# Residual combinations split in product order, a later token scale, and a residual added at the end of the down products

## The chip, the cores and the metric

One core of one Trainium2 chip runs the whole program. The metric is the device time of one execution in microseconds (us); of the kernel before, 3 runs give a median of 2325.0 us (2323.95 to 2326.51).

## What is computed

One layer of an encoder with two branches, for two requests of 256 tokens each (512 tokens in all), width 2048, all in float32. After the mixer (attention heads and a gated delta rule, together y) the layer is

```python
h  = h + mixed                      # mixed = y @ w_out
hn = rmsnorm(h, norm_ffn_w)
h  = h + (silu(hn @ w_gate) * (hn @ w_up)) @ w_down
return rmsnorm(h, final_norm_w)     # x * rsqrt(mean(x*x) + 1e-6) * w
```

with `w_gate` and `w_up` of 2048 x 5632 and `w_down` of 5632 x 2048. The change lies wholly behind the mixer: in the residual after `w_out`, the opening of the gate products, and the `w_down` stage with its residual.

## The kernel before, in words

Activations lie transposed: 128 features on the partitions, 512 tokens (T) along a row, 16 such row tiles for the 2048 features. L = 256 is one request's half of the row.

**Every float32 product is made of three.** A matrix is split into a high part (`hi`, a rounding on ACT, L126) and a low part (`lo`, the difference on DVE, L127). PE multiplies hi by hi, hi by lo and lo by hi. In the matmul rows of the profile `ps_g`, `ps_a` and so on name the PSUM bank, `w_hi` and `w_lo` the weights. All PE code runs in program order; DVE, ACT and POOL run in an order that a scheduler makes from the program order and from leads: code under `high_priority(offset=AHEAD)` is placed as if it stood 120 instructions earlier. The pools allow three raw weight tiles (`raw`), three `hi` and three `lo`, three PSUM banks of tag `g`, three of tag `s`, and one each of `o0` and `o1`.

**The residual stage (L852-877)** runs over 16 row tiles in the order 0, 8, 1, 9 and so on, so that tile j is followed by tile j + 8. Each gets its half of the `w_out` products, the residual is added (L858), the row is stored to memory as `s_h2` (L859), and it is scaled into four blocks (two feature halves by two token halves). From the four blocks seven inputs of a Strassen-like scheme are built: A11, A12, A22 are blocks, S1 to S4 sums and differences (L864-872). They stand in one tile `cmb`, and after row j + 8 all seven are split at once into `XC[j]` (L873, 1792 columns). L877 adds up the squares for the norm's scale.

**Gate and up products.** A block of two feature tiles needs seven products instead of eight: A11, S3, S1, A12, S2, S4, A22 in this order. Each runs over j = 0 to 7 with the eight tiles of `XC`, first all high weights and then all low ones. The weights of a product are blocks b11, b21, b22 of the matrix or their running sums (`first`, `second`, the first addition by an accumulating DMA of POOL, L914). The products A11 and A12 share the bank `ps_a`: between them a copy and an add (L896/L897) read A11 out as `p1`. There are 22 gate blocks and 22 up blocks, alternating. In the first gate block, `open_gate` (L982-994) runs after the product A11: one PE product that sums the squares over all features (`ps_s<-ssq_acc,ones`), a square root on ACT, four reciprocals on DVE (L202), each over 128 columns, and the opening of the pools in which the blocks hold their results. Each block ends with a multiplication by the scale (L977). The results of an up block are stored to memory by POOL (`s_act`, L1011), or kept split in `sA`.

**Down stage.** The 5632 inputs fall into three segments of plain products (`down`, L1041-1055), two groups that use the seven-product scheme (`down_group`, L1093), and a last segment (`down_half`, L1160), one token half after the other with the final norm behind it. The order is down(0), group 0, down(1), group 1, down(2), and the two halves. In `down` each j has one load of 512 KB of weights on SP's queue (`w_raw`), a split, and two row tiles of twelve matmuls; `tt(hk, hk, ps, add)` (L1051) adds the bank to the result's row of `hT`. Beside the j's, `combos` builds the group's inputs (`a_raw`, `a_sum`, split into `xd`). Before down(0) sixteen POOL loads bring the residual `s_h2` into `hT` (L1026-1027); `hT` takes memory that the gate and up blocks used until then, and a tile waits for the last user of its place. PE, DVE and ACT are in-order: what stands behind a waiting instruction waits too.

Of the kernel before, what the change touches and what calls it, by code (L numbers as in the profile page):

```python
# [8 lines left out]
F32 = mybir.dt.float32  # L9
F32R = mybir.dt.float32r  # L10
# [7 lines left out]
P = 128  # L18
# [43 lines left out]
def hybrid_encoder(ctx: ExitStack, tc: tile.TileContext, xT, w_in, w_ba, w_out, w_gate,  # L62
# [786 lines left out]
    st = st_cm.__enter__()  # L849
    acc = st.tile([P, T], F32, tag="acc", name="ssq_acc2")  # L850
    A11, A12, A22, S4, S3, S1, S2 = range(7)
    for n, i in enumerate(pairs):  # L852
        j = i % 8
        ps = pg.tile([P, T], F32, tag="g", name="ps_g")
        hk = st.tile([P, T], F32, tag="hk", bufs=2, name="hk")
        nc.sync.dma_start(hk, s_h1[i])
        half_gemm(ps, w_out[i, 1], dns, True, True)
        tt(hk, hk, ps, ALU.add)  # L858
        nc.gpsimd.dma_start(s_h2[i], hk)  # L859
        w = nwf[:, i:i + 1]  # L860
        if i < 8:
            cmb = st.tile([P, 7, L], F32, tag="cmb", name="cmb")
            a21 = st.tile([P, L], F32, tag="a21", name="a21")
            act(out=cmb[:, A11], in_=hk[:, :L], func=AF.Copy, scale=w)  # L864
            act(out=a21, in_=hk[:, L:], func=AF.Copy, scale=w)
            tt(cmb[:, S3], cmb[:, A11], a21, ALU.subtract)
        else:
            act(out=cmb[:, A12], in_=hk[:, :L], func=AF.Copy, scale=w)
            act(out=cmb[:, A22], in_=hk[:, L:], func=AF.Copy, scale=w)
            tt(cmb[:, S1], a21, cmb[:, A22], ALU.subtract)  # L870
            tt(cmb[:, S2], cmb[:, S1], cmb[:, A11], ALU.subtract)
            tt(cmb[:, S4], cmb[:, A12], cmb[:, S2], ALU.add)
# [45 lines left out]

    def block(src, f, pool, new_out, opened=None):


        with tc.high_priority(offset=3 * AHEAD):
# [19 lines left out]
        fp, out = state["fp"], new_out()  # L942
        p1 = fp.tile([P, L], F32, tag="p1", name="p1")
# [22 lines left out]
        tt(out[:, 3], out[:, 3], d[:, 1], ALU.add)  # L966
        with ahead():
# [3 lines left out]
        with ahead():  # L971
            tt(first, first, b21, ALU.add)
            w = w_split(first)
# [7 lines left out]

    def open_gate():  # L982
        ps = sm_tile()
        mm(ps, ones, acc, start=True, stop=True)
        rstd_bcast(ps, rstd2, st, 1)
        st_cm.__exit__(None, None, None)
        cp_cm.__exit__(None, None, None)
        sA_pool = ctx.enter_context(tc.tile_pool(name="sA", bufs=1, side="left",
                                                 reuse_waits="tile"))
        state["gb_cm"] = tc.tile_pool(name="gB", bufs=1, side="left", reuse_waits="tile")  # L990
        state["gB"] = state["gb_cm"].__enter__()
        state["fp_cm"] = tc.tile_pool(name="fp", bufs=1, side="left", reuse_waits="tile")
        state["fp"] = state["fp_cm"].__enter__()
        state["sA"] = sA_pool.tile([P, 2, SEG, T], F32R, tag="sA", name="aA")

    for p in range(NPAIR):
        g4 = block(w_gate, 2 * p, gA,
                   lambda: state["fp"].tile([P, 4, L], F32, tag="g4", name="ga"),
                   open_gate if p == 0 else None)
        act(out=g4, in_=g4, func=AF.Silu)  # L1000
        u4 = block(w_up, 2 * p, state["gB"],
                   lambda: state["fp"].tile([P, 4, L], F32, tag="u4", bufs=2, name="up"))
        tt(u4, u4, g4, ALU.mult)
        sA = state["sA"]
# [15 lines left out]
    ht = ctx.enter_context(tc.tile_pool(name="ht", bufs=1, side="left", reuse_waits="tile"))  # L1020
    hT = ht.tile([P, KT, T], F32, tag="h", name="hT")

    def hrow(i):
        return hT[:, i]

    for i in range(KT):  # L1026
        nc.gpsimd.dma_start(hrow(i), s_h2[i])
# [4 lines left out]
    sA = state["sA"]  # L1032

# [6 lines left out]

    def down(s, a, beside=()):  # L1041
        beside = list(beside)
        for j in range(8):
            wh, wl = load_w(w_down[s, j], [2, SEG, P])
            for i in range(2):
                ps = pg.tile([P, T], F32, tag="g", name="ps_g") if i == 0 else sm_tile()
                for k in range(SEG):
                    mm3(ps, wh[:, i, k], wl[:, i, k], a[:, 0, k], a[:, 1, k],
                        k == 0, k == SEG - 1)
                hk = hrow(2 * j + i)  # L1050
                tt(hk, hk, ps, ALU.add)  # L1051
            if beside:
# [39 lines left out]

    def down_group(g, X, sums, after):  # L1093
        plain = fetch_plain(g, 0)
        for j in range(8):
# [78 lines left out]
    def final_norm(b, acc):  # L1174
# [122 lines left out]
```

## Time and profile before

| | |
|---|---|
| median of 3 runs | 2325.0 us |
| profiled execution | 2323.5 us, span 2321.8 us, mean granted clock 0.993 |
| busy share of PE, DVE, ACT, POOL | 98%, 77%, 45%, 11% |
| HBM | 357.42 MB read, 36.00 MB written |
| mixer and residual stage | until about 968 us of the span |
| gate and up blocks | about 959 to 1835 us |
| down stage | about 1835 us to the end |

A row of the timeline gives the start and the busy time in us of one or more instructions on an engine (PE matrix products, PEld weight loads, DVE vector, ACT scalar, POOL and SPq the two queues of DMA), the line of the code, what was written from what, and in brackets how long the engine idled before and what ended that. A row of windows gives a stretch's length, the busy time of the five engines with their instruction counts, the share of full clock that PE was granted, the share of the DMA engines' time in use, and GB/s. DMA rows give the issues, their size and the median time to landing.

### The profile page before, as it was taken

The numbers are of one execution on the slowest core, as the hardware profiler recorded it, in microseconds if no ns is written. First come the engines' busy times: TensorE is split into PE (matmuls) and PEld (weight loads), VectorE is DVE, ScalarE is ACT, GpSimd is POOL, SyncE is SP. The second block draws the span as 40 slices with busy tenths as digits, with TensorE's granted clock in tenths as the row PEclk, the third lists the DMA queues.
The fourth block names the chain that finished last, engine by engine and source line by source line (L and its number), as shares of the span: only waits on it lengthen the run. The fifth ranks groups of instructions, "written<-read, shape, count | busy, mean of one in ns | idle before, by whom it ended". The sixth has DMA issues, their size and how long they took to land.

```text
span 2321.8 us, 32492 instructions
## 1 busy us (share of the span) xinstructions
PE 2266.8 (98%) x12260; PEld 1915.1 (82%) x12260; DVE 1779.1 (77%) x2744; ACT 1037.0 (45%) x1566; POOL 245.7 (11%) x382
## 2 busy tenths in 40 slices
PE   8999999999999999899999999999999989999997
PEld 6777788887787788688888888888888778878887
DVE  7644599985566636688888888888888788898876
ACT  6777223234333315444444444444444344444435
POOL 2111200002000011101011010101000111000000
PEclk9999999999999999999999999999999999999999
DMA  5433623247444547567868777777777567767642
GB/s 202 128 122 112 179 94 101 97 115 185 131 128 136 200 143 221 180 177 197 217 190 217 192 214 194 210 198 207 199 196 186 163 233 186 193 184 200 159 155 73
DMA packets 119821, 395.56 MB, mean 170 GB/s; under 512 B 15232, under 2 KB 23328, under 8 KB 118512
## 3 DMA queue, kind: packets, MB, share of 16 engines
q1 hardware_dynamic: 87232, 283.42, 36.2%
q0 software_dynamic: 32432, 110.05, 22.7%
q8 instruction: 97, 1.59, 0.3%
q14 instruction: 60, 0.49, 0.1%
HBM read 357.42 MB, written 36.00 MB: 169 GB/s over the span
## 4 chain that ended last, share of the span: by engine, by line
PE 81%; DVE 12%; DMA 4%; issue 1%; ACT 1%; SPq 0%; DVEq 0%; ACTq 0%
PE ps_g L74 27%; PE ps_d L74 14%; PE ps_a L74 14%; PE ps_c L74 14%; PE ps_b L74 7%; PE ps_s L74 4%; DVE prod L512 3%; DVE W L514 3%; DVE w_lo L127 3%; DMA w_raw<-in_w_down_dram 2%; PE ps_o L74 1%; DMA w_raw<-in_w_in_dram 1%; DMA qg<-s_eg 1%; ACT w_hi L126 1%; PE ps_s L77 1%
## 5 line engine op out<-in xcount | busy, mean ns | idle before, releaser
L74 PE MATMUL ps_g<-xhi,w_hi 128*128 128x512 f32 x896 | 368.3, 411 | 0.0
L74 PE MATMUL ps_g<-xhi,w_lo 128*128 128x512 f32 x896 | 351.5, 392 | 4.4 <-DVE w_lo L127 4.3
L74 PE MATMUL ps_g<-xlo,w_hi 128*128 128x512 f32 x896 | 351.0, 392 | 0.0
L127 DVE TENSOR_TENSOR w_lo<-w_raw,w_hi 128x1024 fp32r<-128x1024 f32 x168 | 205.0, 1220 | 113.2 <-ACT w_hi L126 111.0
L126 ACT ACTIVATE w_hi<-b 128x1024 fp32r<-128x1024 f32 (+1 forms) x180 | 185.7, 1032 | 234.6 <-issue 103.6
L126 ACT ACTIVATE w_hi<-w_raw 128x1024 fp32r<-128x1024 f32 x168 | 177.2, 1056 | 245.2 <-PE ps_g L74 167.4
L126 ACT ACTIVATE w_hi<-w_first 128x1024 fp32r<-128x1024 f32 x132 | 140.0, 1061 | 219.5 <-PE ps_c L74 139.7
L127 DVE TENSOR_TENSOR w_lo<-b,w_hi 128x1024 fp32r<-128x1024 f32 (+1 forms) x180 | 212.7, 1182 | 4.4 <-PE ps_a L74 2.7
L74 PEld LDWEIGHTS ps_g<-xhi,w_lo 128*128 128x128 f32 x896 | 168.8, 188 | 43.3 <-DVE w_lo L127 6.3
L74 PEld LDWEIGHTS ps_g<-xhi,w_hi 128*128 128x128 f32 x896 | 169.1, 189 | 42.7 <-issue 7.4
L74 PEld LDWEIGHTS ps_g<-xlo,w_hi 128*128 128x128 f32 x896 | 169.3, 189 | 30.5 <-issue 0.2
L127 DVE TENSOR_TENSOR w_lo<-w_first,w_hi 128x1024 fp32r<-128x1024 f32 x132 | 161.2, 1221 | 41.3 <-ACT w_hi L126 34.1
L74 PE MATMUL ps_a<-xc,w_hi 128*128 128x512 f32 x704 | 177.7, 394 | 10.9 <-DVE xc L127 7.2
L74 PE MATMUL ps_c<-xc,w_hi 128*128 128x512 f32 x704 | 177.4, 394 | 0.0
L74 PE MATMUL ps_d<-xc,w_hi 128*128 128x512 f32 x704 | 176.3, 392 | 0.0
L74 PEld LDWEIGHTS ps_a<-xc,w_hi 128*128 128x128 f32 x704 | 127.2, 190 | 34.3 <-DVE xc L127 7.6
L74 PEld LDWEIGHTS ps_c<-xc,w_hi 128*128 128x128 f32 x704 | 127.1, 189 | 23.7 <-issue 1.0
L74 PEld LDWEIGHTS ps_d<-xc,w_hi 128*128 128x128 f32 x704 | 126.6, 189 | 22.6
L74 PEld LDWEIGHTS ps_a<-xc,w_lo 128*128 128x128 f32 x704 | 97.8, 194 | 7.0
L74 PEld LDWEIGHTS ps_d<-xc,w_lo 128*128 128x128 f32 x704 | 96.0, 190 | 6.9
L74 PEld LDWEIGHTS ps_c<-xc,w_lo 128*128 128x128 f32 x704 | 96.0, 190 | 6.9
L74 PE MATMUL ps_a<-xc,w_lo 128*128 128x256 f32 x704 | 99.8, 285 | 0.0
(356 smaller groups left out, 4295.8 us busy)
## 6 DMA issues: line engine op xcount, KB each, us to landing
w_raw<-in_w_in_dram SPq DMA_DIRECT2D x112, 512.0 KB, 3.5
b<-in_w_gate_dram SPq DMA_DIRECT2D x66, 512.0 KB, 4.1
b<-in_w_up_dram SPq DMA_DIRECT2D x66, 512.0 KB, 5.5
b<-in_w_group_dram SPq DMA_DIRECT2D x48, 448.0 KB, 4.0
w_raw<-in_w_out_dram SPq DMA_DIRECT2D x32, 512.0 KB, 3.6
w_raw<-in_w_down_dram SPq DMA_DIRECT2D x32, 512.0 KB, 4.2
w_two<-in_w_group_dram SPq DMA_DIRECT2D x32, 448.0 KB, 5.7
w_two<-in_w_group_dram POOLq DMA_DIRECT2D x32, 448.0 KB, 6.8
```

The source lines that it names most:

```text
L74: pin(nc.tensor.matmul(*a, **k))
L77: pin(nc.tensor.transpose(*a))
L126: act(out=hi, in_=src, func=AF.Copy)
L127: tt(lo, src, r32(hi), ALU.subtract)
L512: tt(pv, W[:, s0:s1, s0:c], kkq[:, c, 0, None, s0:c].broadcast_to([P, n, j]), ALU.mult)
L514: nc.vector.tensor_reduce(W[:, s0:s1, c], pv, AX.X, ALU.add)
```

## The change

**Split in product order.** `cmb` becomes two tiles: `top` with A11 and S3, split when row j (below 8) is there, and `low` with S1, A12, S2, S4, A22, split after row j + 8. For the last one, j = 7, `low` is split in three pieces: S1; A12 and S2; S4 and A22. The seven take in `XC` the places in which the products use them. `down_group` keeps the old places.

**Token scale.** The product of the squares, the root and the reciprocals move from behind A11 to behind A12 of the first gate block, as `token_scale`. The pools are opened before the blocks. The splits of that block's last four weights get a lead of 20 instead of 120.

**Residual at the end.** The sixteen loads before down(0) go. `hT` becomes eight tiles of two rows each. down(0) writes its rows with a copy on ACT; down(1) adds as before; down(2) adds, and behind each j one accumulating DMA of POOL (`plus`) adds the two residual rows, 512 KB, to `hT[j]`.

```diff
...
-    A11, A12, A22, S4, S3, S1, S2 = range(7)
+    A11, S3, S1, A12, S2, S4, A22 = range(7)
...
         if i < 8:
-            cmb = st.tile([P, 7, L], F32, tag="cmb", name="cmb")
+            top = st.tile([P, 2, L], F32, tag="top", name="cmb_top")
             a21 = st.tile([P, L], F32, tag="a21", name="a21")
...
-            tt(cmb[:, S3], cmb[:, A11], a21, ALU.subtract)
+            tt(top[:, 1], top[:, 0], a21, ALU.subtract)
+            split(x[:, :S1, 0], x[:, :S1, 1], top)
         else:
...
-            tt(cmb[:, S1], a21, cmb[:, A22], ALU.subtract)
-            tt(cmb[:, S2], cmb[:, S1], cmb[:, A11], ALU.subtract)
-            tt(cmb[:, S4], cmb[:, A12], cmb[:, S2], ALU.add)
-            split(XC[j][:, :, 0], XC[j][:, :, 1], cmb)
+            low = st.tile([P, 5, L], F32, tag="low", name="cmb_low")
+            s1, a12, s2, s4, a22 = [low[:, c] for c in range(5)]
...
+            tt(s1, a21, a22, ALU.subtract)
+            cuts = (0, 1, 3, 5) if j == 7 else (0, 5)
+            for c0, c1 in zip(cuts, cuts[1:]):
+                if c0 <= 2 < c1:
+                    tt(s2, s1, top[:, 0], ALU.subtract)
+                if c0 <= 3 < c1:
+                    tt(s4, a12, s2, ALU.add)
+                split(x[:, S1 + c0:S1 + c1, 0], x[:, S1 + c0:S1 + c1, 1], low[:, c0:c1])
...
+        lead = 20 if scale else AHEAD
...
         product(pa, w, XC, A11, True)
-        if opened:
-            opened()
...
-        with ahead():
+        with ahead(lead):
             w = w_split(b21)
         product(pa, w, XC, A12, False, True)
         plus_both(out[:, 0], None, pa)
-        with ahead():
+        if scale:
+            scale()
+        with ahead(lead):
             tt(first, first, b22, ALU.add)
...
+    def token_scale():
         ps = sm_tile()
         mm(ps, ones, acc, start=True, stop=True)
-        rstd_bcast(ps, rstd2, st, 1)
...
+        sd = fp.tile([P, T], F32, tag="u4", bufs=2, name="sd")
+        act(out=sd, in_=ps, func=AF.Sqrt, scale=1.0 / D, bias=epsc)
+        for i in range(0, T, P):
+            nc.vector.reciprocal(rstd2[:, i:i + P], sd[:, i:i + P])
...
-    hT = ht.tile([P, KT, T], F32, tag="h", name="hT")
+    hT = [ht.tile([P, 2, T], F32, tag=f"h{j}", name="hT") for j in range(8)]
...
-    for i in range(KT):
-        nc.gpsimd.dma_start(hrow(i), s_h2[i])
...
-    def down(s, a, beside=()):
+    def down(s, a, beside=(), first=False, residual=False):
...
-                tt(hk, hk, ps, ALU.add)
+                if first:
+                    nc.scalar.copy(hk, ps)
+                else:
+                    tt(hk, hk, ps, ALU.add)
+            if residual:
+                plus(hT[j], s_h2[2 * j:2 * j + 2].rearrange("i p t -> p i t"))
...
-        down(g, sA, [combos(g, X, n) for n in range(GROUP)])
+        down(g, sA, [combos(g, X, n) for n in range(GROUP)], first=(g == 0))
...
-    down(2, sA)
+    down(2, sA, residual=True)
```

What this makes of the engines' order is seen at three places. On DVE at the opening of the gate products stood this, from the second combination of tile 7 (L871) to the add that frees A11's bank (L897), with `b_8123` and `b_8124` the blocks b21 and b22 of the first gate block:

```order
L871 TENSOR_TENSOR cmb<-cmb 128x256
L877 TENSOR_TENSOR ssq_acc_7412<-ssq_acc_7412,h_sq 128x512
L872 TENSOR_TENSOR cmb<-cmb 128x256
L127 TENSOR_TENSOR xc<-cmb,xc 128x7x256
L127 TENSOR_TENSOR w_lo<-b_8123,w_hi 128x1024
L202 RECIPROCAL rstd_8115<-sd 128x128 x2
L127 TENSOR_TENSOR w_lo<-w_first,w_hi 128x1024
L202 RECIPROCAL rstd_8115<-sd 128x128
L127 TENSOR_TENSOR w_lo<-b_8124,w_hi 128x1024
L972 TENSOR_TENSOR w_first<-w_first,b_8123 128x1024
L202 RECIPROCAL rstd_8115<-sd 128x128
L897 TENSOR_TENSOR p_8173<-p_8173,ps_a 128x256
```

Now this stands there, from the first combination of `low` (L874) to the same add (L905):

```order
L874 TENSOR_TENSOR cmb_low<-a_8084,cmb_low 128x256
L885 TENSOR_TENSOR ssq_acc_7412<-ssq_acc_7412,h_sq 128x512
L878 TENSOR_TENSOR cmb_low<-cmb_low,cmb_top 128x256
L127 TENSOR_TENSOR w_lo<-b_8163,w_hi 128x1024
L127 TENSOR_TENSOR xc<-cmb_low,xc 128x256
L127 TENSOR_TENSOR xc<-cmb_low,xc 128x2x256
L880 TENSOR_TENSOR cmb_low<-cmb_low 128x256
L969 TENSOR_TENSOR w_first<-w_first,b_8164 128x1024
L127 TENSOR_TENSOR xc<-cmb_low,xc 128x2x256
L127 TENSOR_TENSOR w_lo<-w_first,w_hi 128x1024
L905 TENSOR_TENSOR p_8193<-p_8193,ps_a 128x256
```

The one split of 7 x 256 columns became three, of which the first, S1, stands ahead of the last combination, and no reciprocal is left before the add. The reciprocals (L1006) now stand further down, among the weight splits of the gate block's end and of the first up block (`b_8349`, `w_second`):

```order
L1006 RECIPROCAL rstd_8143<-sd 128x128 x2
L127 TENSOR_TENSOR w_lo<-b_8349,w_hi 128x1024
L1006 RECIPROCAL rstd_8143<-sd 128x128
L127 TENSOR_TENSOR w_lo<-w_second,w_hi 128x1024
L1006 RECIPROCAL rstd_8143<-sd 128x128
L907 TENSOR_TENSOR u_8291<-ps_b,p_8193 128x256
L127 TENSOR_TENSOR w_lo<-w_first,w_hi 128x1024
```

And this is what stands ahead of the add that frees the up block's own first bank (`p_8380`), the scale's multiplication L986 included:

```order
L908 TENSOR_TENSOR ga<-ga,ps_c 128x256
L981 TENSOR_TENSOR w_first<-w_first,b_8350 128x1024
L986 TENSOR_TENSOR ga<-ga,rstd_8143 128x1024
L127 TENSOR_TENSOR w_lo<-b_8351,w_hi 128x1024
L905 TENSOR_TENSOR p_8380<-p_8380,ps_a 128x256
```

The third place is POOL's queue around down(0), where `w_two` are the sums of the group's weights and `s_act` the stores of the up blocks. Before:

```order
L1011 DMA s_act<-up 128x1024
L914 DMA w_two<-in_w_group_dram 128x896
L1011 DMA s_act<-up 128x1024
L914 DMA w_two<-in_w_group_dram 128x896 x2
L1027 DMA hT<-s_h_103 128x512 x16
L914 DMA w_two<-in_w_group_dram 128x896
L1038 DMA aA<-s_act 128x1024 x2
L914 DMA w_two<-in_w_group_dram 128x896 x16
```

Now, to the end of the program:

```order
L1022 DMA s_act<-up 128x1024
L922 DMA w_two<-in_w_group_dram 128x896 x3
L1046 DMA aA<-s_act 128x1024 x2
L922 DMA w_two<-in_w_group_dram 128x896 x16
L1046 DMA aA<-s_act 128x1024 x2
L922 DMA w_two<-in_w_group_dram 128x896 x12
L1046 DMA aq<-s_act 128x1024 x2
L922 DMA hT<-s_h_103 128x2x512 x8
```

The sixteen loads are gone from ahead of the weight sum, and eight accumulating ones stand at the queue's end, behind the activations of the last segment (`aq`).

More of the change, by code (lines that the diff above doesn't have):

```diff
@@ L849, in hybrid_encoder @@
     st = st_cm.__enter__()
-    acc = st.tile([P, T], F32, tag="acc", name="ssq_acc2")
-    A11, A12, A22, S4, S3, S1, S2 = range(7)
+    acc = gA.tile([P, T], F32, tag="acc", name="ssq_acc2")
+    A11, S3, S1, A12, S2, S4, A22 = range(7)
     for n, i in enumerate(pairs):
@@ L860, in hybrid_encoder @@
         w = nwf[:, i:i + 1]
+        x = XC[j]
         if i < 8:
-            cmb = st.tile([P, 7, L], F32, tag="cmb", name="cmb")
+            top = st.tile([P, 2, L], F32, tag="top", name="cmb_top")
             a21 = st.tile([P, L], F32, tag="a21", name="a21")
-            act(out=cmb[:, A11], in_=hk[:, :L], func=AF.Copy, scale=w)
+            act(out=top[:, 0], in_=hk[:, :L], func=AF.Copy, scale=w)
             act(out=a21, in_=hk[:, L:], func=AF.Copy, scale=w)
-            tt(cmb[:, S3], cmb[:, A11], a21, ALU.subtract)
-        else:
-            act(out=cmb[:, A12], in_=hk[:, :L], func=AF.Copy, scale=w)
-            act(out=cmb[:, A22], in_=hk[:, L:], func=AF.Copy, scale=w)
-            tt(cmb[:, S1], a21, cmb[:, A22], ALU.subtract)
-            tt(cmb[:, S2], cmb[:, S1], cmb[:, A11], ALU.subtract)
-            tt(cmb[:, S4], cmb[:, A12], cmb[:, S2], ALU.add)
-            split(XC[j][:, :, 0], XC[j][:, :, 1], cmb)
+            tt(top[:, 1], top[:, 0], a21, ALU.subtract)
+            split(x[:, :S1, 0], x[:, :S1, 1], top)
+        else:
+            low = st.tile([P, 5, L], F32, tag="low", name="cmb_low")
+            s1, a12, s2, s4, a22 = [low[:, c] for c in range(5)]
+            act(out=a22, in_=hk[:, L:], func=AF.Copy, scale=w)
+            act(out=a12, in_=hk[:, :L], func=AF.Copy, scale=w)
+            tt(s1, a21, a22, ALU.subtract)
[6 more added lines that the diff above has]
+                split(x[:, S1 + c0:S1 + c1, 0], x[:, S1 + c0:S1 + c1, 1], low[:, c0:c1])
         sq = acc if n == 0 else st.tile([P, T], F32, tag="sq", name="h_sq")
@@ L907, in w_split, with ahead @@
         return hi, lo
-    def ahead():
-        return tc.high_priority(offset=AHEAD)
+    def ahead(lead=AHEAD):
+        return tc.high_priority(offset=lead)
     def plus(dst, src):
@@ L917, in bank, with block @@
         return pool_.tile([P, T], F32, tag=tag, name=nm).rearrange("p (a t) -> p a t", a=2)
-    def block(src, f, pool, new_out, opened=None):
+    def block(src, f, pool, new_out, scale=None):
         with tc.high_priority(offset=3 * AHEAD):
@@ L939, in block @@
         product(pa, w, XC, A11, True)
-        if opened:
-            opened()
-        fp, out = state["fp"], new_out()
+        out = new_out()
         p1 = fp.tile([P, L], F32, tag="p1", name="p1")
@@ L966, in block @@
         tt(out[:, 3], out[:, 3], d[:, 1], ALU.add)
-        with ahead():
+        with ahead(lead):
             w = w_split(b22)
@@ L970, in block @@
         plus_both(out[:, 2], u2, pd, ALU.subtract)
-        with ahead():
+        with ahead(lead):
             tt(first, first, b21, ALU.add)
@@ L980, in hybrid_encoder @@
     rstd2 = gA.tile([P, T], F32, tag="rstd2", name="rstd2")
-    def open_gate():
+    st_cm.__exit__(None, None, None)
+    cp_cm.__exit__(None, None, None)
+    sA_pool = ctx.enter_context(tc.tile_pool(name="sA", bufs=1, side="left", reuse_waits="tile"))
+    gb_cm = tc.tile_pool(name="gB", bufs=1, side="left", reuse_waits="tile")
+    gB = gb_cm.__enter__()
+    fp_cm = tc.tile_pool(name="fp", bufs=1, side="left", reuse_waits="tile")
+    fp = fp_cm.__enter__()
+    sA = sA_pool.tile([P, 2, SEG, T], F32R, tag="sA", name="aA")
+    def token_scale():
         ps = sm_tile()
         mm(ps, ones, acc, start=True, stop=True)
-        rstd_bcast(ps, rstd2, st, 1)
[L986 to L994, printed above, removed]
+        sd = fp.tile([P, T], F32, tag="u4", bufs=2, name="sd")
+        act(out=sd, in_=ps, func=AF.Sqrt, scale=1.0 / D, bias=epsc)
+        for i in range(0, T, P):
+            nc.vector.reciprocal(rstd2[:, i:i + P], sd[:, i:i + P])
     for p in range(NPAIR):
         g4 = block(w_gate, 2 * p, gA,
-                   lambda: state["fp"].tile([P, 4, L], F32, tag="g4", name="ga"),
-                   open_gate if p == 0 else None)
+                   lambda: fp.tile([P, 4, L], F32, tag="g4", name="ga"),
+                   token_scale if p == 0 else None)
         act(out=g4, in_=g4, func=AF.Silu)
-        u4 = block(w_up, 2 * p, state["gB"],
-                   lambda: state["fp"].tile([P, 4, L], F32, tag="u4", bufs=2, name="up"))
+        u4 = block(w_up, 2 * p, gB,
+                   lambda: fp.tile([P, 4, L], F32, tag="u4", bufs=2, name="up"))
         tt(u4, u4, g4, ALU.mult)
-        sA = state["sA"]
         if p in SEG_PAIRS[0]:
@@ L1011, in hybrid_encoder @@
             nc.gpsimd.dma_start(s_act[p], u4.rearrange("p a t -> p (a t)"))
-    state["fp_cm"].__exit__(None, None, None)
-    state["gb_cm"].__exit__(None, None, None)
+    fp_cm.__exit__(None, None, None)
+    gb_cm.__exit__(None, None, None)
     ga_cm.__exit__(None, None, None)
@@ L1093, in down_group @@
     def down_group(g, X, sums, after):
+        A11, A12, A22, S4, S3, S1, S2 = range(7)
         plain = fetch_plain(g, 0)
@@ L1102, in down_group @@
                 after()
-            h = hT[:, 2 * j:2 * j + 2].rearrange("p f (b t) -> p (f b) t", b=2)
+            h = hT[j].rearrange("p f (b t) -> p (f b) t", b=2)
             pa, pb = bank(pg, "g", "ps_a"), bank(pso, "o0", "ps_b")
@@ L1192, in final_norm @@
             if k % 2:
-                nc.sync.dma_start(y[b, k // 4, :, k % 4 - 1:k % 4 + 1], hT[:, k - 1:k + 1, t0:t1])
+                nc.sync.dma_start(y[b, k // 4, :, k % 4 - 1:k % 4 + 1], hT[k // 2][:, :, t0:t1])
                 yield
```

3 lines of the change are left out of this document (1 added, 2 removed).

## The prediction

> **What bounds the kernel now.** The page comes first: the busy times, then what PE, the engine at 98%, waits for.
>
> ```profile
> span 2321.8 us, 32492 instructions
> PE 2266.8 (98%) x12260; PEld 1915.1 (82%) x12260; DVE 1779.1 (77%) x2744; ACT 1037.0 (45%) x1566; POOL 245.7 (11%) x382
> ```
>
> The chain of waits of PE (columns: what waited, for what; us in total, times, longest):
>
> ```profile
> PE ps_g L74 <- DVE hT L1051: 7.6, 1, 7.6
> PE ps_a L74 <- DVE xc L127: 7.2, 1, 7.2
> PE ps_a L74 <- DVE p L897: 3.7, 1, 3.7
> ```
>
> PE idles 55.0 us in all, and three waits that come once each hold 18.5 of it. Two stand where the gate/up products open, one where the down stage opens: the two places that the change edits. No matmul is removed (the mean-square product only moves), so the gain can only be these waits and what follows from them. The timeline of the first place (start, busy us, engine, line, operation, out<-in, count, and in brackets the idle time before it and what ended it):
>
> ```profile
> 959.13 1.75 PE L74 MATMUL ps_a<-xc,w_hi 128*128 128x512 f32 x7
> 959.34 0.69 DVE L858 TENSOR_TENSOR hk<-hk,ps_g 128x512 f32<-128x512 f32 x1 [0.75 <-PE ps_g L74]
> 960.21 1.23 DVE L127 TENSOR_TENSOR w_lo<-w_first,w_hi 128x1024 fp32r<-128x1024 f32 x1 [0.18 <-ACT w_hi L126]
> 961.35 0.42 DVE L870 TENSOR_TENSOR cmb<-a,cmb 128x256 f32<-128x256 f32 x1
> 964.26 1.70 ACT L126 ACTIVATE xc<-cmb 128x1792 fp32r<-128x1792 f32 x1 [2.78 <-DVE cmb L872]
> 965.99 2.02 DVE L127 TENSOR_TENSOR xc<-cmb,xc 128x1792 fp32r<-128x1792 f32 x1 [1.82 <-ACT xc L126]
> 968.07 0.80 PE L74 MATMUL ps_a<-xc,w_hi 128*128 128x512 f32 x1 [7.19 <-DVE xc L127]
> 970.37 1.91 PE L74 MATMUL ps_s<-ssq_acc,ones 128*128 128x512 f32 x2
> 974.38 1.76 DVE L202 RECIPROCAL rstd<-sd 128x128 f32<-128x128 f32 x2 [2.48 <-ACT sd L200]
> 981.42 0.36 DVE L897 TENSOR_TENSOR p<-p,ps_a 128x256 f32<-128x256 f32 x1
> 981.84 2.89 PE L74 MATMUL ps_a<-xc,w_hi 128*128 128x512 f32 x8 [3.74 <-DVE p L897]
> 1000.26 2.00 PE L74 MATMUL ps_d<-xc,w_hi 128*128 128x512 f32 x8
> 1003.05 2.00 PE L74 MATMUL ps_a<-xc,w_hi 128*128 128x512 f32 x8
> ```
>
> Seven of A11's eight high products run at once; the eighth needs the last tile j = 7, which is split only when all seven combinations stand (964.26, then 965.99). Then A12 needs the bank of A11 read out by the add at 981.42, which DVE's queue holds behind the reciprocals. Both waits are followed by a slow clock, as the windows show (stretch, length, five engines' busy time, granted clock, DMA share, GB/s):
>
> ```profile
> 968.00:972.00 4.00, 3.93 (x12) 2.88 (x12) 1.24 (x2) 1.06 (x1) 0.00 (x0) 0.50 1.07 212
> 981.80:986.20 4.40, 4.36 (x16) 3.82 (x17) 0.58 (x1) 1.06 (x1) 0.00 (x0) 0.63 0.50 160
> ```
>
> The second place, with the same stage of the second group (2034) as its measure; the last three rows are windows, and the two landing times are those of the down weights in 1830-1895 and in 2020-2080:
>
> ```profile
> 1835.47 0.63 PE L74 MATMUL ps_g<-aA,w_hi 128*128 128x512 f32 x2
> 1852.72 1.06 ACT L126 ACTIVATE w_hi<-w_raw 128x1024 fp32r<-128x1024 f32 x1 [6.04 <-DMA w_raw<-in_w_down_dram]
> 1852.72 1.64 POOL L1027 DMA_DIRECT2D hT<-s_h  x3 [4.23 <-DMA s_act<-up]
> 1858.77 0.69 DVE L1051 TENSOR_TENSOR hT<-hT,ps_g 128x512 f32<-128x512 f32 x1 [3.40 <-DMA hT<-s_h]
> 1859.60 1.19 PE L74 MATMUL ps_g<-aA,w_hi 128*128 128x512 f32 x2 [7.63 <-DVE hT L1051]
> 1874.71 0.73 PE L74 MATMUL ps_g<-aA,w_hi 128*128 128x512 f32 x2 [2.12 <-ACT w_hi L126]
> 1895.07 1.75 PE L74 MATMUL ps_a<-xd,w_hi 128*128 128x512 f32 x7
> 2034.01 0.63 PE L74 MATMUL ps_g<-aA,w_hi 128*128 128x512 f32 x2
> 2080.25 1.75 PE L74 MATMUL ps_a<-xd,w_hi 128*128 128x512 f32 x7
> DMA to landing us min/median/max: 3.4/5.5/9.1
> DMA to landing us min/median/max: 3.2/4.3/5.5
> 1852.00:1868.00 16.00, 8.40 (x29) 6.81 (x30) 8.89 (x12) 3.91 (x4) 8.96 (x17) 0.79 1.04 350
> 1868.00:1895.00 27.00, 22.41 (x93) 16.66 (x92) 22.05 (x32) 10.84 (x12) 1.08 (x2) 1.00 0.68 214
> 2240.00:2262.00 22.00, 22.00 (x104) 18.41 (x103) 16.82 (x18) 9.39 (x10) 0.00 (x0) 1.00 0.52 168
> ```
>
> The residual loads start only at 1852.72, when their memory is free, the adds wait for them, three PSUM banks fill, and PE stands for 7.63 us.
>
> **Part 1, the split order and the token scale.** From 959.13 to the up block's A12 at 1003.05 are 43.92 us. A product takes 1003.05 - 1000.26 = 2.79 us; ten of them (seven of the gate block, three of the up block) and the mean-square product (1.91 at clock 0.50, so 0.96 at full) make 28.9. So 15.0 us are excess: 7.19 + 3.74 = 10.9 of waits and 4.1 of slow clock.
>
> After the change A11 and S3 of tile 7 are split eight steps of the loop earlier, so both products run from 959.13 to 964.7 without a wait. S1 needs a 256-column split; on DVE stand before it, after the residual add (until 960.03), one w_lo (1.23), two 256-column steps (0.42 each), the square add (0.69, a 512-column step like the residual add) and w_lo of b21 (1.2): 964.0, and 0.4 for the split itself, whose high half ACT has ready. Products go tile by tile and tile 7 is the eighth: no wait. S1 ends at 967.5. A12 accumulates into A11's bank, so the add p must be done. The twelve DVE rows from w_lo to that add are three weight splits and one weight sum (1.22 each, 4.9), five 256-column steps (2.0, with p at 0.36) and three 512-column steps (2.0): 8.9, so 969.0. **A wait of 1.5 us** takes the place of 3.74, and that for the split is gone. The mean-square product ends at 972.8, and the first reciprocal comes 2.1 later as now (970.37 + 1.91, then 974.38), at 974.9. S2, S4, A22 and three products of the up block follow: its A12 could start at 972.8 + 6 x 2.79 = 989.5.
>
> Here is the new cost. DVE is behind: from the first reciprocal to the up block's p it has 21 rows: the reciprocals (twice 1.76, 3.5), six weight splits, two weight sums and the rstd product (nine at 1.22, 11.0), and nine of 256 columns (3.7): 18.2, so 993.1. Where DVE doesn't wait, a row starts 0.09 before the one ahead ends (960.21 + 1.23 against 961.35), which would take 1.8 off: 991.3. I take 992.3, nearer the middle. **So the up block's A12 waits 2.8 us.** It comes at 992.3 instead of 1003.05: **10.8 saved** before any clock loss. The bounds: 13.5 if nothing but the first 1.5 stays, 7 if DVE is held 3.8 us more (its reciprocals once again, about what further waits in its queue could add). On the clock: the waits of 7.19 and 3.74 were followed by 0.50 and 0.63, the one of 2.12 at 1874.71 by 1.00. A wait of 2.8 lies between: 0 to (1 - 0.63) x 4.4 = 1.6; I take 0.6.
>
> The Trainium skill, in "TensorE: Matmul & The Clock Gate", section "HAM oscillation — how this bites in real kernels", asks for PE gaps of no more than some 3.4 us: by it the 2.8 us wait is free, and the time would be 0.6 lower. The three waits above agree with it.
>
> **Part 2, plain copies.** Stage one of the down phase takes 1895.07 - 1835.47 = 59.60 us before, and 2080.25 - 2034.01 = 46.24 in the second group, with the same products: 13.4 excess. It is 7.63 of wait, 27.00 - 22.41 = 4.6 idle after 1868, and the rest clock. The sixteen loads go (4.2 MB, in a stretch where DMA is at 1.04), and the adds become copies on ACT, which need only PSUM. They take 0.57 or so each (an estimate from the row below); ACT is busy 3.91 of 16 there, and 16 DVE adds of 0.69 go.
>
> ```profile
> 978.40 0.59 ACT L949 COPY p<-ps_c 128x512 f32<-128x512 f32 x1
> ```
>
> What is late next is the weight of j = 3. PE is there at 1852.0 (1859.60 - 7.63); its high half starts at 1852.72 after its own DMA, whose rivals until then (SwiGLU stores, group sums, activations) all stay: it is done at 1853.8, 1.8 us late, and the low half 1.2 later, of which I count all: 3.0. The copies of tiles j = 4 and 5 now wait for a store of the last products; it landed at 1852.72 and they come from 1857 on, so it is free. After that I expect landings as in 2020-2080. **Saved 13.4 - 3.1 = 10.3.** Bounds: 13.4 (as the second group), and 7.63 - 3.0 = 4.6 if the idle time after 1868 stays.
>
> **Part 3, the residual by DMA.** The same 4.2 MB come back as eight accumulating loads of 512 KB on POOL's queue in the last plain stage, one behind each j. The first add of the final half products follows:
>
> ```profile
> 2224.69 0.68 DVE L1051 TENSOR_TENSOR hT<-hT,ps_s 128x512 f32<-128x512 f32 x1
> 2262.42 0.42 DVE L1171 TENSOR_TENSOR hT<-hT,ps_g 128x256 f32<-128x256 f32 x1 [0.31 <-PE ps_g L74]
> 2263.86 0.42 DVE L1171 TENSOR_TENSOR hT<-hT,ps_g 128x256 f32<-128x256 f32 x1 [1.02 <-PE ps_g L74]
> w_first<-in_w_up_dram POOLq DMA_DIRECT2D x22, 512.0 KB, 8.9
> q0 software_dynamic: 32432, 110.05, 22.7%
> ```
>
> Load 0 can go at 2225.4, load 7 behind the last add, just ahead of 2262.4. The consumer takes two rows per j at 1.44 each, so tile j is wanted at 2262.4 + 2.88 j, the last at 2282.6. An accumulating load lands in 8.9 us in the slowest row of the page: the last at 2271, 11 us early, and POOL's busy time there is 0.00. Bandwidth: 22.7% of 2321.8 us for 110.05 MB is 4.8 us of all engines per MB, so 4.2 MB are 20 us; on the 46 us from 2225.4 to 2271 that is 0.44 on top of 0.52. It is tight, but the weights are fetched three buffers ahead. **Zero**, with a loss as the other bound (below). The tail is unchanged.
>
> **Sum.** The profiled execution: 2323.5 - 10.8 + 0.6 - 10.3 = 2303.0. It lies 1.5 under the median (span 2321.8 and 1.7 around it); for the median, 2325.0 - 20.5 = **2304.5**. A measurement tells some 0.2% (4.6 us) from no change.
>
> **The rivals.** *Weights bound the down stage* (0.16): part 2 gives 4.6, so 2310.2. For it speaks the weight wait of 2.12 at 1874.71, after the loads; against it the second group, which has the same weights. *DVE bounds the opening* (0.12): its queue is held longer, part 1 gives 7 less 0.6, and the time is 2308.3. For it: its queue has no slack from 960 to 992; against: PE waited for none of its weight splits here before. *Both openings close fully* (0.09): 13.5 and 13.4, 2298.1. *The residual stalls the end, slower than before*: if the accumulating loads run one after the other, each P long, tile 7 stands at 2225.4 + 8P, wanted at 2282.6 plus 2.9, two free PSUM banks of 1.44. It decides from P = 7.5 on; at 8.9 PE loses 11.1 (2315.6, chance 0.04), and from P = 10.7 the 20.5 and 4.6 are gone: at P = 11, 28 lost and 2332 (0.06). For it: the row of 8.9, and the 0.98; against: from 1852 to 1868, with the sixteen residual loads in POOL's queue, the engines moved 350 GB/s, 5.6 MB, though without adding. The Trainium skill speaks for it in "DMA: Bandwidth & Descriptors", section "Issuing engines are not separate DMA queues": GpSimd's loads run on the same 16 engines as SyncE's, so they have no lane of their own; the full share of 1.04 with both queues active agrees. *It does not do what it says* (0.06): weights or the copies' PSUM still stop PE as long, part 2 and part 1 give 2 each, 2321.
>
> **The numbers.** My forecast holds 0.47 with its own range 2300 to 2308. With 0.16, 0.12 and 0.09 beside it, 2297 to 2315 holds 0.84. Faster: 0.47 + 0.16 + 0.12 + 0.09 + 0.04 = 0.88; same 0.06; slower 0.06.
>
> **What would show it.** Right: no wait of ps_a for xc at the opening; one of 1 to 2 us for p in the gate block and of 2 to 4 in the up block; 30 to 35 us from the first A11 to the up block's A12; the first down stage in 48 to 51 us, its only wait for weights; the accumulating loads landed by 2272 less the gain, no wait for hT in the tail. Wrong: an opening that waits for the reciprocals or for S1's split, copies that wait on ACT's queue, weight landings over 6 us in the last stage, or a PE wait at L1171's place.

## The result, and the profile after

The changed kernel takes 2312.6 us (median of 4 runs, 2310.42 to 2315.47), the kernel before 2325.8 (4 runs); the ratio is 0.9937, 95% interval 0.9926 to 0.9949. The profiled execution of the changed kernel took 2314.4 us, span 2312.3. The gain is 13.1 us where 20.5 were forecast: the time lies above the forecast's own range of 2300 to 2308 and within the wider one of 2297 to 2315, so the size is what has to be explained. The waits of PE at the places that the change edits (in total, times, longest):

```profile
PE ps_g L74 <- DVE hT L1062: 3.2, 1, 3.2
PE ps_a L74 <- DVE xc L127: 2.6, 1, 2.6
PE ps_a L74 <- ACT ga L1012: 2.6, 1, 2.6
PE ps_a L74 <- DVE p L905: 0.8, 1, 0.8
```

The 7.6 for the residual loads is gone, and the 7.2 for the split has become 2.6, which was to be nothing. The 2.6 for `ga` is the up block's A12, and the 0.8 the gate block's. A wait of 3.2 for the last plain stage's adds is new. The stages, from the starts of PE's rows (A11's first row, the first plain row of a down stage, the first product of a group, the first row of the half products, the final sum):

| stage | before | after | change |
|---|---|---|---|
| until A11 | 959.13 | 959.35 | +0.2 |
| opening: A11 to S2 of the first up block | 46.72 | 41.55 | -5.2 |
| other gate and up blocks | 829.62 | 829.82 | +0.2 |
| down(0) | 59.60 | 50.66 | -8.9 |
| group 0 | 138.94 | 136.99 | -2.0 |
| down(1), group 1, down(2) | 226.78 | 227.11 | +0.3 |
| half products | 48.50 | 54.44 | +5.9 |
| final norm to the end | 12.51 | 12.38 | -0.1 |

The opening in the timeline:

```profile
956.36 1.27 ACT L126 ACTIVATE xc<-cmb_low 128x1280 fp32r<-128x1280 f32 x1 [1.61 <-DVE cmb_low L880]
957.66 1.49 DVE L127 TENSOR_TENSOR xc<-cmb_low,xc 128x1280 fp32r<-128x1280 f32 x1 [1.40 <-ACT xc L126]
959.07 1.22 DVE L127 TENSOR_TENSOR w_lo<-w_second,w_hi 128x1024 fp32r<-128x1024 f32 x1
959.35 1.75 PE L74 MATMUL ps_a<-xc,w_hi 128*128 128x512 f32 x7
960.21 0.68 DVE L858 TENSOR_TENSOR hk<-hk,ps_g 128x512 f32<-128x512 f32 x1
962.99 0.69 DVE L127 TENSOR_TENSOR xc<-cmb_top,xc 128x512 fp32r<-128x512 f32 x1
963.59 0.68 DVE L858 TENSOR_TENSOR hk<-hk,ps_g 128x512 f32<-128x512 f32 x1
963.73 0.78 PE L74 MATMUL ps_a<-xc,w_hi 128*128 128x512 f32 x1 [2.64 <-DVE xc L127]
972.68 0.41 DVE L905 TENSOR_TENSOR p<-p,ps_a 128x256 f32<-128x256 f32 x1
973.15 2.11 PE L74 MATMUL ps_a<-xc,w_hi 128*128 128x512 f32 x8 [0.84 <-DVE p L905]
996.69 2.70 PE L74 MATMUL ps_a<-xc,w_hi 128*128 128x512 f32 x8 [2.56 <-ACT ga L1012]
1000.90 2.21 PE L74 MATMUL ps_b<-xc,w_hi 128*128 128x512 f32 x8
```

A11 of the gate block waits for the top split of tile 7. That split hangs on row 7's add, which stands at 960.21; row 15's add follows at 963.59, 4.25 us later than the 959.34 of before. No add waits for PE here: DVE is behind. From there every row to the up block's A12 (996.69 instead of the forecast 992.3) is late by about that much.

The first plain stage and the end, where the last two rows are windows:

```profile
1830.72 0.63 PE L74 MATMUL ps_g<-aA,w_hi 128*128 128x512 f32 x2
1848.47 0.73 PE L74 MATMUL ps_g<-aA,w_hi 128*128 128x512 f32 x2 [1.24 <-ACT w_hi L126]
1857.11 0.73 PE L74 MATMUL ps_g<-aA,w_hi 128*128 128x512 f32 x2 [2.09 <-ACT w_hi L126]
1881.38 1.75 PE L74 MATMUL ps_a<-xd,w_hi 128*128 128x512 f32 x7
2241.21 1.06 ACT L126 ACTIVATE wd<-w_raw 128x1024 fp32r<-128x1024 f32 x1 [4.67 <-DMA w_raw<-in_w_down_dram]
2242.30 1.23 DVE L127 TENSOR_TENSOR wd<-w_raw,wd 128x1024 fp32r<-128x1024 f32 x1 [3.91 <-ACT wd L126]
2250.86 0.68 DVE L1062 TENSOR_TENSOR hT<-hT,ps_g 128x512 f32<-128x512 f32 x1
2251.69 6.49 PE L74 MATMUL ps_g<-aq,wd 128*128 128x256 f32 x31 [3.17 <-DVE hT L1062]
2224.00:2246.00 22.00, 22.00 (x101) 18.30 (x100) 11.70 (x13) 7.01 (x7) 3.56 (x3) 1.00 0.97 236
2251.69:2258.00 6.31, 6.31 (x31) 6.31 (x32) 3.91 (x8) 3.02 (x7) 1.20 (x1) 0.54 0.87 130
```

The first stage waits only for its weights, as forecast. At the end the DMA share is 0.97 instead of 0.52. Weights of the half products arrive late, one after the other (the first is shown): ACT and then DVE wait for them, and the adds behind their splits in DVE's queue keep PE's banks full. PE loses 3.17 us, and runs the next 6.31 us at 0.54 of its clock, which is 2.9 more.

### The profile page after: what moved, and what is told of

Its sections match the earlier page's. It is cut to its first block, busy times and chain, and to the rows that moved or that the text cites. A ratio compares the mean times of both kernels' runs of the same rounds, so it can differ in the third digit from the quotient of the medians.

```text
span 2312.3 us, 32529 instructions
## 1 busy us (share of the span) xinstructions
PE 2269.0 (98%) x12260; PEld 1919.8 (83%) x12260; DVE 1770.8 (77%) x2738; ACT 1046.6 (45%) x1592; POOL 245.7 (11%) x374
## 4 chain that ended last, share of the span: by engine, by line
PE 82%; DVE 11%; DMA 4%; issue 2%; ACT 1%; POOL 0%; SPq 0%; DVEq 0%; ACTq 0%; POOLq 0%
PE ps_g L74 27%; PE ps_a L74 14%; PE ps_d L74 14%; PE ps_c L74 14%; PE ps_b L74 7%; PE ps_s L74 4%; DVE prod L512 3%; DVE W L514 3%; DVE w_lo L127 2%; DMA w_raw<-in_w_down_dram 2%; PE ps_o L74 1%; DMA w_raw<-in_w_in_dram 1%; PE ps_s L77 1%; DMA qg<-s_eg 1%; ACT w_hi L126 1%
## 5 line engine op out<-in xcount | busy, mean ns | idle before, releaser
L126 ACT ACTIVATE w_hi<-w_two 128x896 fp32r<-128x896 f32 x64 | 60.9, 952 | 86.6 <-PE ps_c L74 37.5
```

The source lines that it names most:

```text
L126: act(out=hi, in_=src, func=AF.Copy)
```

## The experiments

Twelve kernels, every one timed against runs of the kernel before on its own chip (medians 2326.2 to 2327.7 there). Ratios to the kernel before compare them (the changed kernel: 0.9937); single stages are read from the profiles. The interval is about 0.0013 to either side, 3 us. A stage of one profile is surer than that: the opening takes 41.55 to 42.46 us in the seven kernels that share the changed kernel's code there, and down(0) 50.15 to 52.13 in the eleven with the copies on ACT. The half products with the loads beside them are less so.

| kernel | us | ratio, interval | opening | down(0) | half products |
|---|---|---|---|---|---|
| changed | 2312.64 | 0.9937 (0.9926-0.9949) | 41.55 | 50.66 | 54.44 |
| e_split | 2321.15 | 0.9971 (0.9960-0.9983) | 42.04 | 59.72 | 48.51 |
| e_down | 2319.96 | 0.9971 (0.9961-0.9980) | 46.51 | 52.13 | 54.09 |
| e_late | 2307.59 | 0.9913 (0.9899-0.9927) | 36.34 | 50.31 | 52.54 |
| e_early | 2316.56 | 0.9951 (0.9939-0.9963) | 42.73 | 51.85 | 51.46 |
| e_actscale | 2311.68 | 0.9941 (0.9928-0.9953) | 38.57 | 51.20 | 51.30 |
| e_nores | 2307.35 | 0.9911 (0.9897-0.9924) | 42.30 | 50.65 | 48.50 |
| e_plain | 2309.17 | 0.9931 (0.9917-0.9944) | 42.03 | 50.15 | 48.51 |
| e_resgroup | 2310.54 | 0.9923 (0.9911-0.9936) | 42.02 | 50.54 | 48.51 |
| e_tailpin | 2315.15 | 0.9944 (0.9933-0.9956) | 41.80 | 51.00 | 52.30 |
| e_dvecopy | 2319.92 | 0.9969 (0.9957-0.9981) | 42.46 | 54.14 | 52.28 |
| e_lateres | 2304.11 | 0.9897 (0.9884-0.9909) | 36.34 | 50.85 | 48.50 |
| e_combo | 2301.24 | 0.9898 (0.9885-0.9912) | 33.22 | 51.96 | 48.51 |

**The parts alone.** e_split takes back the third part: the loads return and the copies become adds.

```diff
+    for i in range(KT):
+        nc.gpsimd.dma_start(hrow(i), s_h2[i])
...
-        down(g, sA, [combos(g, X, n) for n in range(GROUP)], first=(g == 0))
+        down(g, sA, [combos(g, X, n) for n in range(GROUP)])
...
-    down(2, sA, residual=True)
+    down(2, sA)
```

> Only the first two parts of the change (split order and token scale); the residual loads stand ahead of the down stage and its adds on DVE, as before the change, though in eight tiles. Theory: the opening gives 5.0 us, the down stage none: 2320.8. Rival: the opening's gain is lost again at the down stage, because the early products only reach the same late loads sooner: within 2 us of the 2325.8 before.

e_down is the kernel before up to the gate and up blocks' end, with the changed kernel's down stage behind it.

> Only the third part of the change: copies in the first plain stage, no residual loads ahead of it, accumulating loads in the last plain stage; the opening of the gate products as before the change. Theory: the first plain stage and the group behind it take 50.7 + 137.0 us instead of 59.6 + 138.9 (10.9 saved), the last plain stage and the last products lose 5.9 of it again, so about 5 us are left: 2320.8. Rival: with the down stage starting 5 us later than in the changed kernel its loads meet other traffic, and the loss at the end or the gain at the start is gone: 2315 (no loss) or 2325 (no gain).

Both theories held: 0.9971 each, so 0.0029 twice, against 0.0063 together. As far as the interval tells, the two parts don't touch each other. And the gain and the loss of the third part stand in one kernel: in e_down the first stage is 7.5 us shorter than before, group 0 2.0 shorter, and the half products 5.6 longer.

**The late row.** e_late swaps the low split and the next row's add, in every turn of the residual stage. ACT's half of the split moves with DVE's, and `pin` keeps an instruction at its place in the program order:

```diff
...
+    late = []
...
-        tt(hk, hk, ps, ALU.add)
+        pin(tt(hk, hk, ps, ALU.add))
+        while late:
+            hi, lo, src = late.pop()
+            act(out=hi, in_=src, func=AF.Copy)
+            pin(tt(lo, src, r32(hi), ALU.subtract))
...
-                split(x[:, S1 + c0:S1 + c1, 0], x[:, S1 + c0:S1 + c1, 1], low[:, c0:c1])
+                piece = (x[:, S1 + c0:S1 + c1, 0], x[:, S1 + c0:S1 + c1, 1], low[:, c0:c1])
+                if j == 7:
+                    split(*piece)
+                else:
+                    late.append(piece)
```

> The changed kernel, with one swap on DVE in the residual stage: the add of the next row (L858) stands ahead of the low split of the tile before, instead of behind it. Theory: the opening's missing gain is a late row. DVE reaches row 15's add only at 963.59 us, 4.2 us after PE has finished the row, because the splits wait for ACT inside DVE's queue; with the swap the add comes within 0.5 us of PE's end, the wait of A11 for its split (2.64) goes, A12 of the gate block starts about 4 us earlier after A11's start (9.8 us instead of 13.8), and the median falls by 4, to about 2308.6. Rival: A11 waits for ACT's part of the split, which stands in ACT's queue wherever the add is; then a wait of 2 us or more stays and the time is within 1 us of 2312.6.

```profile
956.08 0.69 DVE L859 TENSOR_TENSOR hk<-hk,ps_g 128x512 f32<-128x512 f32 x1 [1.61 <-PE ps_g L74]
956.68 1.49 DVE L863 TENSOR_TENSOR xc<-cmb_low,xc 128x1280 fp32r<-128x1280 f32 x1
961.32 1.07 PE L74 MATMUL ps_a<-xc,w_hi 128*128 128x512 f32 x4
961.52 0.69 DVE L859 TENSOR_TENSOR hk<-hk,ps_g 128x512 f32<-128x512 f32 x1 [0.48 <-PE ps_g L74]
971.23 2.12 PE L74 MATMUL ps_a<-xc,w_hi 128*128 128x512 f32 x8 [1.40 <-DVE p L914]
994.78 2.08 PE L74 MATMUL ps_a<-xc,w_hi 128*128 128x512 f32 x8 [2.54 <-DVE p L914]
994.78:997.66 2.88, 2.88 (x17) 2.53 (x17) 0.46 (x1) 0.74 (x2) 0.00 (x0) 1.00 0.77 265
```

The last row is a window. The adds now wait for PE, as before the change, and A11 waits for nothing. The gate's A12 comes 9.91 us after A11 (forecast 9.8), its wait is 1.40 (forecast 1.5); the up block's A12 comes at 33.46 (forecast 33.2) with a wait of 2.54 (forecast 2.8). The opening is 5.2 us shorter than in the changed kernel: the up block's A12 comes 3.9 us earlier after A11, and the product behind its wait takes 2.88 us instead of 4.21, at full clock. The theory holds.

**Where the scale stands.** e_early puts it back behind A11:

```diff
         product(pa, w, XC, A11, True)
+        if scale:
+            scale()
...
-        if scale:
-            scale()
```

> The changed kernel with the token scale back behind the product A11 (the split order stays). Theory: the four reciprocals (3.7 us) only change their place in DVE's queue: now they stand ahead of the gate block's add p, so A12 there waits some 4 us longer, while the up block's A12 (2.56, with 1.4 of slow clock) waits for nothing; the opening is 0 to 2 us longer and the time 2312 to 2315. Rival: the later place is most of the gain: the opening loses 4 us or more, over 2316.

The up block's wait goes, and the gate block's A12 waits 3.50 for p instead of 0.84. The opening is 1.2 us longer than in the changed kernel, within the theory. The median is over 2316, but on a chip where the kernel before takes 2327.7; by the ratio it is 2314.4 beside 2325.8, and the two intervals overlap. So the move of the scale by itself is worth little, 1.2 us in the opening and by the times nothing that is clear of the interval; the reciprocals are paid at one A12 or the other. e_actscale takes them off DVE:

```diff
-        act(out=sd, in_=ps, func=AF.Sqrt, scale=1.0 / D, bias=epsc)
-        for i in range(0, T, P):
-            nc.vector.reciprocal(rstd2[:, i:i + P], sd[:, i:i + P])
+        act(out=sd, in_=ps, func=AF.Ln, scale=1.0 / D, bias=epsc)
+        act(out=rstd2, in_=sd, func=AF.Exp, scale=-0.5)
```

> The changed kernel with the four reciprocals on DVE (3.7 us) replaced by a logarithm and an exponential on ACT. Theory: the wait of the up block's A12 for its add p (2.56, and 1.4 of slow clock behind it) is DVE's queue, in which the reciprocals stand: the wait falls under 0.5 and the time by 3 to 4 us, to about 2309. Rival: the queue is held by what waits for ACT, and ACT gets two more operations and table loads: the wait stays at 2 us or more and the time within 1 us of 2312.6.

In the profile the theory holds: the up block's A12 waits for nothing and the opening is 3.0 us shorter. The time doesn't show it: 0.9941, where the theory had some 2309 us. A gain of 3 us is at the edge of the interval.

**The end.** e_nores leaves the eight loads out.

```diff
-    down(2, sA, residual=True)
+    down(2, sA)
```

> The changed kernel with the eight accumulating residual loads left out, so the residual is missing from the output. Theory: the loads fill the DMA engines (share 0.97 instead of 0.53), the down weights land late, their splits hold up DVE's queue, and the adds behind them hold up PE: without the loads the wait of PE for the add (3.17) goes, the clock stays at 1.00 at the start of the last products, the landing median of the down weights is 3.6 again, and about 5.5 us are saved: 2307. Rival: the wait comes from the new tiles or the order of the last stage and not from the traffic: then a wait of about 3 us stays, within 1.5 us of 2312.6.

The half products take 48.50 us as before the change, there is no wait for the adds, and the eleven down weights that are fetched from the start of down(2) on land in 3.5 instead of 7.1 us (medians; 4.2 before the change). So the loads cause the loss. Whether by their bytes or by the addition, e_plain asks:

```diff
-                plus(hT[j], s_h2[2 * j:2 * j + 2].rearrange("i p t -> p i t"))
+                junk = lp.tile([P, 2, T], F32, tag="junk", bufs=2, name="junk")
+                nc.gpsimd.dma_start(junk, s_h2[2 * j:2 * j + 2].rearrange("i p t -> p i t"))
```

> The changed kernel with the eight accumulating loads replaced by plain POOL loads of the same rows into a tile that nobody reads, so the residual is missing from the output; the same 4.2 MB at the same places without the addition. Theory: it is the bytes that fill the DMA engines: the share stays above 0.85, the wait at the start of the last products at 2 to 3 us, the time at 2310 to 2313. Rival: it is the addition that is expensive (the destination is read too): share near 0.75, no wait, 2307 as with no loads at all.

My theory fell. The same bytes without the addition cost PE nothing, at a share of 0.80 and 0.74 in the two halves of the stage (48.51 us; the time, 0.9931, shows less of that than the profile does, and lies between the changed kernel and e_nores). The software queue from 2202 to 2262, first in the changed kernel, then in e_plain (packets, MB, share of 16 engines):

```profile
q0 software_dynamic: 2464, 5.24, 50.2%
```

```profile
q0 software_dynamic: 1440, 5.24, 25.3%
```

Both have the eight loads and 1.05 MB of plain activations. Plain, 25.3% of 60 us is 15.2 us for 5.24 MB, 2.9 us per MB; with 3.0 us off for the activations, the accumulating 4.19 MB take 27.1, 6.5 us per MB, 2.2 times as much. The packets say the same: 1024 more for the same bytes, 128 for each load. The Trainium skill says of the ReduceScatter collective ("Collectives: The Full Stack", section "The bandwidth ceiling: the fold count and why AG ≠ RS ≠ AR") that its addition needs two source reads, and gives a measured ratio of 1.93 between a plain gather and it. The 2.2 here is of that size, though on another path, and no run here shows the reads themselves. One thing isn't separate: the plain loads don't wait for the adds, so they also came earlier. The weights beside them landed in 4.5 us. e_resgroup moves the accumulating loads:

```diff
+            if g == 1:
+                plus(hT[j], s_h2[2 * j:2 * j + 2].rearrange("i p t -> p i t"))
...
-    down(2, sA, residual=True)
+    down(2, sA)
```

> The changed kernel with the eight accumulating loads behind the eight steps of the second group instead of the last plain stage; the same bytes in 137 us instead of 44. Theory: the tail's wait goes (5.5 us saved, about 2307), and the group, with a DMA share of 0.7 and weights fetched a step ahead, stays at 137.0 us. Rival: the contention moves along: the group's weight sums queue behind the loads on POOL, PE waits there for 3 us or more, and the time stays at 2310 to 2314.

Beside group 1 they are free: 136.98 us for the group at a share of 0.78, and 48.51 for the half products. The median of 2310.5 looks like the rival's, but its kernel before took 2327.4: by the ratio it is 2307.9, and the group doesn't wait. Its interval overlaps the changed kernel's, so that the move pays is read from the profile. e_tailpin leaves them and fixes DVE's order instead, adds ahead of splits:

```diff
...
-                else:
-                    tt(hk, hk, ps, ALU.add)
+                elif residual:
+                    pin(tt(hk, hk, ps, ALU.add))
...
+            act(out=keep[0][:, j], in_=raw, func=AF.Copy)
+            pin(tt(keep[1][:, j], raw, r32(keep[0][:, j]), ALU.subtract))
...
+    down(2, sA, [lambda: None] * 5 + [lambda j=j: load_half(j) for j in range(8)], residual=True)
```

> The changed kernel with DVE's order at the end of the last plain stage fixed: an add never stands behind more than the splits of the half products' weights that its own step can spare (the weights of the halves are split behind the steps 5, 6 and 7 and after). The accumulating loads stay where they are. Theory: PE waits because its adds stand behind splits whose weights land late; with the adds ahead the wait of 3.2 us goes, the weights, wanted only from the half products on, are in time, and 4 to 5.6 us are saved: 2307 to 2308.6. Rival: the weights themselves are too late under that traffic: PE waits the same 3 us or more for them a few us later, 2311 to 2315.

```profile
2253.60 1.06 ACT L1180 ACTIVATE wd<-w_raw 128x1024 fp32r<-128x1024 f32 x1 [4.11 <-DMA w_raw<-in_w_down_dram]
2254.69 1.22 DVE L1181 TENSOR_TENSOR wd<-w_raw,wd 128x1024 fp32r<-128x1024 f32 x1 [1.76 <-ACT wd L1180]
2255.83 1.08 DVE L1194 TENSOR_TENSOR hT<-hT,ps_g 128x256 f32<-128x256 f32 x3
2256.30 5.93 PE L74 MATMUL ps_g<-aq,wd 128*128 128x256 f32 x35 [2.06 <-DVE hT L1194]
```

The wait for the plain stage's adds went. PE waits 2.06 us instead for the half products' own adds, behind the next late split, and goes on 6.5 us after the start of the half products (2249.77 here), where it went on 6.2 us after it in the changed kernel. The rival holds: under that traffic it is the weights that are late; the order only chooses who waits.

**The copies.** e_dvecopy puts them on DVE.

```diff
-                    nc.scalar.copy(hk, ps)
+                    nc.vector.tensor_copy(hk, ps)
```

> The changed kernel with the sixteen plain copies of the first plain stage on DVE instead of ACT. Theory: the stage is held by its weights and the residual loads were what mattered, so the engine of the copy does not: the stage takes 50 to 51.5 us and the time stays within 1.5 us of 2312.6. Rival: DVE, busier than ACT there, holds the copies behind its splits: PE waits for PSUM banks, the stage takes 53 us or more.

The rival holds in its size: down(0) takes 54.14 us, group 0 138.91 with its old wait for `hT` (1.75 before), 5.4 us more in the two.

```profile
1910.06 1.86 PE L74 MATMUL ps_d<-xd,w_hi 128*128 128x512 f32 x7 [1.69 <-DVE hT L1154]
```

Its mechanism does not show: in down(0) PE waits for no bank, but 6.1 us in all for weights and their splits, where it waits 4.6 in the changed kernel. Group 0 is the clearer half. It takes 136.98 or 136.99 us in all eleven kernels with the copies on ACT, and 138.77 to 138.94 in the three with DVE in their place. So of the 10.9 us that the third part saves there, the group's 2.0 hang on the copy's engine and not on the loads, and so do some 2 to 4 of the stage's, by the spread of that stage.

**Together.** e_lateres is e_late with the loads of e_resgroup, e_combo has the scale on ACT as well.

> Two mends: the next row's add ahead of the low split, and the residual loads beside the second group; the reciprocals stay on DVE. Theory: 5.2 + 5.6 from 2312.6, 2301.8, with the up block's wait of 2.5 us still there, and 1 to 3 us behind the kernel with all three mends (2301.2). Rival: the scale on ACT is worth nothing in time, as its two table loads delay ACT's splits elsewhere: then it is equal or faster, 2299 to 2301.

> Three mends in one kernel that computes all: the next row's add ahead of the low split, the residual loads beside the second group, the scale on ACT. Theory: the costs lie in different places and add up, 5.2 + 5.6 + 2.5 from the 2312.6 of the changed kernel: 2299.3. Rival: PE meets the next late thing, the weights of the opening or the first plain stage, and a third of it is lost: 2303 to 2305.

By their ratios they take 2301.8 and 2302.1 beside 2325.8. The mends add up in the profiles: an opening of 36.34 and 33.22 us, half products of 48.50 and 48.51. Both kernels beat the changed one, by 0.0040, 9 us. Between them the times can't tell, 0.9897 and 0.9898, so neither e_lateres's theory nor its rival is decided; e_combo lies between its theory and its rival. In the profiles e_combo's span is 1.0 us shorter: of the 3.1 in the opening, 1.1 is lost in down(0), 0.5 ahead of A11 and 0.5 behind the final sum.

## Why the prediction was right in its direction and short in its size

**Part 1** was forecast at 10.8 less 0.6 for the clock and gave 5.2. The step that failed is its first time: "after the residual add (until 960.03)". I took row 15's add from the trace of before, where it waits for PE, and counted what stands behind it. In the new order DVE's own turn in the residual stage had become as long as PE's. The stage's third add before the change, the same add in the changed kernel, and its add of row 6:

```profile
889.60 0.69 DVE L858 TENSOR_TENSOR hk<-hk,ps_g 128x512 f32<-128x512 f32 x1 [2.55 <-DMA hk<-s_h]
893.61 0.69 DVE L858 TENSOR_TENSOR hk<-hk,ps_g 128x512 f32<-128x512 f32 x1 [2.37 <-DMA hk<-s_h]
949.20 0.68 DVE L858 TENSOR_TENSOR hk<-hk,ps_g 128x512 f32<-128x512 f32 x1
```

Two successive adds of the same half stand 11.0 us apart (949.20, and 960.21 for row 7), and two `w_out` rows on PE take 10.9. So DVE never makes good the 4 us that it is behind at the third add, which stands behind a load. In every turn DVE's queue holds two waits for ACT, 1.40 us ahead of that add (as at 957.66) and 0.97 behind it. That cost 4.2 us. e_late, which moves the split with the 1.40 behind the add, shows it: with the add in time all that was worked out behind it holds within 0.3 us. The rival that DVE bounds the opening came nearest: it allowed 3.8 us for further waits in DVE's queue and gave 6.4 for this part. The 0.6 for the clock was 1.4.

**Part 2** was forecast at 10.3 and gave 8.9 in the stage and 2.0 in the group behind it. The waits left are the weights', as said, 1.24 and 2.09 at the j's. What I had put down to the loads alone belongs in part to the copies' engine (e_dvecopy), which I counted as a mere price of 0.57. The group's 2.0 stood in no term of the forecast, so that the two make 10.9 beside 10.3 is luck.

**Part 3** was forecast at zero and cost 5.9 in the profiled execution. The arithmetic gave a share of 0.96 over the 46 us; measured were 0.85 over the 46 us from the first load, and 0.97 in the 22 us up to the half products. That it is near is luck: the 4.8 us per MB were the mean of a queue that mixes plain and accumulating loads, where accumulating ones cost 6.5. The failed step is what followed: "It is tight, but the weights are fetched three buffers ahead". Under that load the median landing time of the weights fetched from the start of down(2) on rose from 4.2 to 7.1 us, over the 6 us that the forecast named as a sign of being wrong, and their splits stand in the same queue as the adds that free PE's banks. The rival that the residual stalls the end had the right place and the wrong mechanism: no add waited for a residual tile. That loss differs from profile to profile, 2.8 to 5.9 us in the seven with the loads in that stage, with waits of 2.1 to 3.8 us and the clock behind them.

Together: -5.2 + 0.2 + 0.2 - 8.9 - 2.0 + 0.3 + 5.9 - 0.1 is the span's -9.5 up to rounding. The medians differ by 13.1, for the profiled execution of the changed kernel is 1.8 us slower than its median, and that of the kernel before 2.3 faster. So the profiles make the shortfall some 4 us larger than the times do. Which stage these 4 us belong to isn't shown; the loss at the end, which differs most between profiles and is largest in the changed kernel's, can hold a part of them.

## What to carry to other kernels

When a change splits one long operation into several, look at the whole turn of the loop and not only at its last pass: an in-order engine that waits for another one in every turn can fall behind by a fixed amount, and every later edge inherits it. A transfer that is moved to where the engines have room must be priced as the operation that it becomes there, and its room judged by the landing time of the stream beside it that is wanted most. A stall that is chased through a queue by reordering returns at the next late input.

## What the runs showed of the hardware that I had not expected

A wait of PE of about 2.5 us was followed by a slow clock in some profiles and not in others. The up block's A12 waited 2.5 to 2.6 us in nine profiles, the changed kernel's among them. In six of them the product behind it took 4.2 to 4.4 us, 1.4 to 1.6 more than its 2.79; in three, e_late among them (clock 1.00), 2.87 or 2.88. What sets the two apart isn't shown. In the changed kernel:

```profile
996.69:1000.90 4.21, 4.21 (x17) 3.70 (x17) 0.46 (x1) 1.06 (x2) 0.00 (x0) 0.65 0.65 219
```

By the Trainium skill's rule of no PE gaps over some 3.4 us ("TensorE: Matmul & The Clock Gate", section "HAM oscillation — how this bites in real kernels") this wait would be free. Six of the nine profiles differ, and so does the wait of 3.17 us with 0.54 behind it: the measurement decides.
